# The fifth gate tile of a first SwiGLU, made as a block pair

## The chip, the core and the metric

The kernel runs on one core of one Trainium2 chip. The metric is the device time of one execution in microseconds (us). One execution is also recorded by the hardware profiler; the numbers of engines, lines and instructions below come from that record.

## The reference, cut to what matters

The reference is a network of two layers over 256 latent tokens and 256 context tokens of width 1024, all in 32-bit floats. Each layer has a SwiGLU, a mixer (a short convolution in layer 0, attention in layer 1) and a second SwiGLU, each behind a modulated norm and ahead of a gated residual. The change lies in the first SwiGLU of layer 0:

```python
def _swiglu(h, w13, w2):
    gte, up = jnp.split(h @ w13, 2, axis=-1)
    return (jax.nn.silu(gte) * up) @ w2

lat = lat + 0.5 * mod[:, 0, 2] * _swiglu(_modulate(lat, norm_g[i, 0], ...), ffn_w13[i, 0], ffn_w2[i, 0])
cx = cx + 0.5 * modc[0, 2] * _swiglu(_modulate(cx, norm_g[i, 0], ...), ffn_w13[i, 0], ffn_w2[i, 0])
```

`w13` is 1024 x 5632, `w2` is 2816 x 1024. Latent and context tokens go through the same weights and lie side by side as 512 columns.

## The kernel before, in words

Every 32-bit operand is split into a high part (ScalarE, a copy with rounding) and a low part (VectorE, the source minus the high part). A product is three matmuls: high by high, high weight by low operand, low weight by high operand (`mm3`, L148 to L150 of the profile).

The hidden width is cut into 22 gate tiles of 128, 11 in each half `t` of `ffn`. A tile's weights are 128 x 2048: eight blocks of 128 rows of the contraction, for gate and for up. A tile is made in one of two ways.

**Plain tile.** For each of the 8 contraction blocks, gate and up, three matmuls over all 512 columns: 48 matmuls of 512. Its weights are split in two instructions of 1024 columns on ScalarE and two on VectorE (`load_w`). `w13_post` then makes silu(gate) on ScalarE, the product with up on VectorE, and the two parts of the result.

**Block pair** (class `Pair`). The tile is taken as a 2 x 2 block product (contraction halves by gate and up, against contraction halves by latent and context columns) in Winograd's form with seven products in place of eight: 84 matmuls of 256 columns. It needs weight sums, made by VectorE in the raw weight tile: `sub(0)`, `sub(1)`, `sub(2)` (L804, L809, L811), and four groups of split weights: A (1024 columns), A22 (512), S12 (1024), S34 (1024), each with a ScalarE conversion (L786) and a VectorE one (L789). Of the operand it needs its eight blocks, which are there, and four block sums T1 to T4, split too. In the first SwiGLU they are made once, by `FirstBlocks.sums` (L404 to L411; conversions at L123 and L124), in two pieces of 512 columns each.

The pair loop runs in a fixed order on PE, VectorE and ScalarE (`manual_schedule`): what stands first in the code goes first on its engine. What is written before the loop is placed by the framework's scheduler, which goes by written order among what is ready; `tc.issue_after(x)` adds that an instruction of x's engine comes after x. Iteration `i` of the loop makes, for pair `i`: `head` (products A11 and A12), `five` (S1 by T1), `six` (S2 by T2, S4 by an operand block, then VectorE's add at L847); and for the pair before it `seven` (S3 by T3), which comes between `five` and `six`, and `four` (A22 by T4), which comes last. Among them stand the weights of the next pair: A22 and `sub(0)` after `head`, A and `sub(1)`, `sub(2)` after `seven`, the conversions of S12 and S34 on ScalarE after `six`. The low parts of S12 and S34 are VectorE's first two instructions of the next iteration. ScalarE copies partial results out of the accumulator at L834 (in `head`), L840 (in `five`) and L844 (in `six`).

Split weights lie in four buffers of 1024 columns (`half`), raw weights in two (`load_raw`, filled from SyncE's queue).

In the first SwiGLU, tiles 0 to 2 are made in the hand-ordered start of the kernel, tiles 3 and 4 are plain, and pairs 5 to 10 follow in the loop; the second half `t = 1` is all pairs. `PLAIN` says how many tiles of a SwiGLU are plain. Between their other work the stages also spread 224 "units" of the modulation weights (VectorE, L167, `tick`): `tick(n)` adds n to an account, and each whole one issues a unit. A loop iteration with a pair before it adds `PER_PAIR` = 0.7.

Of the kernel before, what the change touches and what calls it, by code (L numbers as in the profile page):

```python
# [15 lines left out]
ALU = mybir.AluOpType  # L16
# [6 lines left out]
T2 = 2 * S  # L23
NM = 22
NH = NM // 2

PLAIN = {(0, 0): 5, (0, 1): 3, (1, 0): 3, (1, 1): NM}
HEADS = 8
KVH = 2
EPS = 1e-6  # L30
# [18 lines left out]
def hybrid_kernel(ctx: ExitStack, tc: tile.TileContext, a: dict, out: bass.AP):  # L49
    nc = tc.nc  # L50
# [70 lines left out]
    def split(hi, lo, src):  # L121
        return (
            nc.scalar.activation(out=hi, in_=src, func=AF.Copy),  # L123
            nc.vector.tensor_tensor(out=lo, in0=src, in1=hi.bitcast(F32), op=ALU.subtract),  # L124
        )
# [251 lines left out]
    class FirstBlocks(Blocks):  # L377
# [8 lines left out]
        def blk(self, key, k):  # L386
            if key[0] == "B":
                return self.h.at(4 * key[1] + k, key[2] * S, key[2] * S + S)
            return super().blk(key, k)

        def sums(self):
            r = self.raw
            tt = nc.vector.tensor_tensor
            for key in ("T1", "T2", "T3", "T4"):
                self.t[key] = hot("th"), hot("tl")

            def keep(key, q, src):
                hi, lo = self.t[key]
                c = slice(q * T2, q * T2 + T2)
                split(hi[:, c], lo[:, c], src)  # L400

            b = lambda hf, s, q: r[2 * hf + q, s]
            for q in range(2):
                tt(out=b(0, 0, q), in0=b(0, 1, q), in1=b(0, 0, q), op=ALU.subtract)  # L404
                keep("T1", q, b(0, 0, q))
            for q in range(2):
                tt(out=b(0, 1, q), in0=b(1, 1, q), in1=b(0, 1, q), op=ALU.add)
                tt(out=b(1, 1, q), in0=b(1, 1, q), in1=b(0, 0, q), op=ALU.add)
                keep("T2", q, b(1, 1, q))
            for q in range(2):  # L410
                tt(out=b(1, 0, q), in0=b(1, 0, q), in1=b(1, 1, q), op=ALU.subtract)  # L411
                keep("T3", q, b(0, 1, q))
            for q in range(2):
                keep("T4", q, b(1, 0, q))

    def new_pair(s):

# [290 lines left out]
    def w13_post(pp, g, c0, c1):  # L708
        n = c1 - c0
        sg = tp.tile([P, T2], F32, name=nm("sg"), tag="sg", bufs=3)  # L710
        nc.scalar.activation(out=sg[:, :n], in_=pp[0][:, :n], func=AF.Silu)
        gm = tp.tile([P, T2], F32, name=nm("gm"), tag="gm", bufs=3)
        nc.vector.tensor_tensor(out=gm[:, :n], in0=sg[:, :n], in1=pp[1][:, :n], op=ALU.mult)
        split(g[0][:, c0:c1], g[1][:, c0:c1], gm[:, :n])
# [36 lines left out]
    class Pair:  # L751
# [34 lines left out]
            nc.scalar.activation(out=self.shaped(g, 0), in_=self.part(g), func=AF.Copy)  # L786

        def lo(self, g):
            nc.vector.tensor_tensor(  # L789
                out=self.shaped(g, 1), in0=self.part(g), in1=self.shaped(g, 0).bitcast(F32),  # L790
                op=ALU.subtract,
            )
# [177 lines left out]
    def ffn(l, b, h, gate, norm, gs=(), ev=1.5, bd=None):  # L970
        gs = list(gs)
        i0 = 0
        n = NH
        for t in range(2):
            between = ()
            with tc.manual_schedule(engines=set(QUEUES[:3])) if bd else nullcontext():
                if bd:
                    gs, first, post = border_ffn(l, b, h, bd)
                for i in range(len(gs), PLAIN[l, b] if t == 0 and not bd else 0):
                    w = load_w(a["w13"][l, b, i])  # L980
                    pp = psum("pg"), psum("pu")
                    w13_mm(pp, w, h, range(KT), 0, T2)
                    gs.append(new_pair("g"))
                    w13_post(pp, gs[-1], 0, T2)
                    if "T1" not in h.t:
                        with tc.issue_after(begun[-1].ins):
                            h.sums()
                i1 = PLAIN[l, b] if bd else len(gs)
                prs = {i1: first} if bd else {}

                def pair(i):
                    if i not in prs and i < n:
                        prs[i] = Pair(a["w13"][l, b, i0 + i], h)
                    return prs.get(i)

                if not bd:
                    pair(i1).both("A")
                    pair(i1).sums(0)
                    pair(i1).sums(1)
                pair(i1 + 1)  # L1000
                prev = done = None
                if bd:
                    prev = post
                with nullcontext() if bd else tc.manual_schedule(engines=set(QUEUES[:3])):
                    for i in range(i1, n):
                        pr, nxt = pair(i), pair(i + 1)
                        if i > i1:
                            pr.lo("S12")
                            pr.lo("S34")
                        elif bd:  # L1010
                            pr.lo("S12")
                            pr.hi("S34")
                            pr.lo("S34")
                        pair(i + 2)
                        ask_ahead()
                        if prev:
                            prev.silu()
                        pr.head()
                        if done:
                            done.gate()  # L1020
                        if nxt:
                            nxt.both("A22")
                            nxt.sub(0)
                        if done:
                            done.gate_parts()
                        if not nxt:
                            tick(1)
                        if bd and i == i1:
                            h.hi("T4")
                            h.lo("T4")  # L1030
                        pr.five()
                        if prev:
                            tick(0 if bd and i == i1 else PER_PAIR if nxt else PER_PAIR + 1)
                            prev.seven()
                        if nxt:
                            nxt.both("A")
                            nxt.sub(1)
                            nxt.sub(2)
                        pr.six()
                        if nxt:  # L1040
                            nxt.hi("S12")
                            nxt.hi("S34")
                        if prev:
                            gs.append(new_pair("g"))
                            prev.four(gs[-1])
                        done, prev = prev, pr
                prev.silu()
                done.gate()
                done.gate_parts()
            bd = None  # L1050

            def last():
                gs.append(new_pair("g"))
                prev.four(gs[-1])
                prev.gate()
                prev.gate_parts()

            between = prev.seven, last
            i0 += n
            raws2 = {}  # L1060

            def ws2(m):
                for i in range(m, min(m + 2, KT)):
                    if i not in raws2:
                        raws2[i] = load_raw(a["w2h"][l, b, t, i], n * P)
                hs = []
                for c0, c1 in ((0, 6 * P), (6 * P, n * P)):
                    hi, lo = half()
                    hs.append((hi, lo))
                    split(hi[:, : c1 - c0], lo[:, : c1 - c0], raws2[m][:, c0:c1])  # L1070

                def at(k):
                    o = (k % 6) * P
                    return tuple(t[:, o : o + P] for t in hs[k // 6])

                return at

            cur = gs
            end = t == 1
            out = project(  # L1080
                ws2, lambda k, c0, c1: (cur[k][0][:, c0:c1], cur[k][1][:, c0:c1]), n,
                gate, ev, between, norm if end else None,
            )
            gs = []
        return out

    h = Plain()
# [263 lines left out]
    with tc.manual_schedule(engines=set(QUEUES)):  # L1351
# [28 lines left out]
        for i in range(3):  # L1380
# [6 lines left out]
            out=sb1, in0=modb[:, 0, KT : 2 * KT], scalar1=1.0, scalar2=None, op0=ALU.add  # L1387
# [100 lines left out]
        for ch in HALVED:  # L1488
            b = modb[:, :, ch * KT : ch * KT + KT]
# [3 lines left out]
    h = FirstBlocks(h, h32)  # L1493
# [5 lines left out]
    bd = ffn(0, 0, h, gate_at(0, 0), (0, 1, hn), gs0, 3.3)  # L1499
    h = hn  # L1500
# [42 lines left out]
    for m in range(KT):  # L1543
# [12 lines left out]
        if m == 0:  # L1556
# [4 lines left out]
            out=d, in0=u, scalar1=convk[:, 1, m : m + 1], scalar2=None, op0=ALU.mult  # L1561
# [4 lines left out]
            out=d2[:, :, 1:], in0=u2[:, :, : S - 1], scalar=convk[:, 0, m : m + 1],  # L1566
            in1=d2[:, :, 1:], op0=ALU.mult, op1=ALU.add,
        )
        nc.vector.scalar_tensor_tensor(
            out=d2[:, :, : S - 1], in0=u2[:, :, 1:], scalar=convk[:, 2, m : m + 1],  # L1570
            in1=d2[:, :, : S - 1], op0=ALU.mult, op1=ALU.add,
# [20 lines left out]
    h = Blocks()  # L1592
# [764 lines left out]
```

## Time and profile before

| | |
|---|---|
| device time, median of 3 runs | 1546.12 us (1545.3 to 1546.77) |
| device time of the profiled execution | 1545.29 us |
| its span, first to last instruction | 1543.4 us |
| PE matmul busy | 1537.9 us (100%) |
| VectorE busy | 1312.7 us (85%) |
| ScalarE busy | 762.9 us (49%) |
| granted TensorE clock | 1.000 |

Matmuls are pipelined: a matmul of 256 columns shows 283 ns although the next one starts earlier, so rates are read from starts and not from durations. Rows of the timeline give start, duration, engine, line, operation, output <- inputs and shape; a bracket at the end is the idle time of the engine before the row and what ended it. `x2` is two instructions merged into a row.

### The profile page before, as it was taken

What the parts mean: (1) busy time and instruction counts of PE and PEld (TensorE: products, weight loads), DVE (VectorE), ACT (ScalarE), POOL (GpSimd) and SP (SyncE); (2) the same over time, 40 slices, a digit from 0 to 9 for tenths busy, and PEclk for the clock granted to TensorE, in tenths of its full rate; (3) what the DMA queues carried; (4) which work ended last, traced back from release to release, by engine and by line L of the source; (5) the groups of instructions that cost most, each with busy time, mean ns of one, the idle gap of its engine ahead of it and who ended that gap; (6) DMA issues with size and microseconds to landing.
All of it is one profiled execution on the core that took longest, in us unless ns stands there. A gap on an engine that the chain in (4) does not pass through costs nothing.

```text
span 1543.4 us, 25345 instructions
## 1 busy us (share of the span) xinstructions
PE 1537.9 (100%) x10250; PEld 1413.6 (92%) x10250; DVE 1312.7 (85%) x1955; ACT 762.9 (49%) x1286; POOL 28.9 (2%) x24
## 2 busy tenths in 40 slices
PE   9999999999999999999999999999999999999999
PEld 7899899989888899988999899988999899998888
DVE  6988889988988799987998989987998877887663
ACT  5554255536223375532554485522554465775551
POOL 0000000000000000000000000000000002220000
PEclk9999999999999999999999999999999999999999
DMA  9434633354565423355333633356334744255561
GB/s 359 137 111 131 214 120 123 123 197 159 191 199 197 164 90 116 115 183 194 124 124 129 214 117 115 115 182 236 133 132 171 267 143 132 103 182 193 189 227 70
DMA packets 52005, 247.72 MB, mean 160 GB/s; under 512 B 6064, under 2 KB 9264, under 8 KB 36656
## 3 DMA queue, kind: packets, MB, share of 16 engines
q1 hardware_dynamic: 51600, 245.91, 46.9%
q8 instruction: 80, 1.31, 0.3%
q14 instruction: 37, 0.30, 0.1%
q10 hardware_dynamic: 288, 0.19, 0.0%
HBM read 243.72 MB, written 1.05 MB: 159 GB/s over the span
## 4 chain that ended last, share of the span: by engine, by line
PE 91%; DVE 4%; DMA 2%; issue 1%; ACT 0%; DVEq 0%; ACTq 0%
PE py L148 9%; PE py L149 9%; PE py L150 9%; PE p L148 7%; PE p L150 7%; PE p L149 7%; PE q L150 5%; PE q L148 5%; PE q L149 5%; PE py L2015 3%; PE pu L2015 3%; PE pg L2015 3%; DMA wm<-in_modT 2%; DVE junk L167 2%; DVE wl L124 1%
## 5 line engine op out<-in xcount | busy, mean ns | idle before, releaser
L167 DVE CUSTOM_DVE_ANT_0 junk<-wm,scbc,cst 128x1024 bf16<-128x1024 f32 x224 | 286.8, 1280 | 35.4 <-DMA wm<-in_modT 33.5
L123 ACT ACTIVATE wh<-wr 128x1024 fp32r<-128x1024 f32 (+1 forms) x196 | 177.1, 924 | 204.6 <-PE py L149 129.5
L124 DVE TENSOR_TENSOR wl<-wr,wh 128x1024 fp32r<-128x1024 f32 (+1 forms) x196 | 205.2, 1058 | 41.6 <-PE pg L2015 14.3
L148 PE MATMUL py<-gh,wh 128*128 128x512 f32 (+1 forms) x594 | 217.8, 367 | 0.0
L149 PE MATMUL py<-gl,wh 128*128 128x512 f32 (+1 forms) x594 | 217.3, 366 | 0.0
L150 PE MATMUL py<-gh,wl 128*128 128x512 f32 (+1 forms) x594 | 217.1, 365 | 0.0
L786 ACT ACTIVATE wh<-wr 128x1024 fp32r<-128x1024 f32 x165 | 169.5, 1056 | 85.4 <-DVE wr L809 62.9
L789 DVE TENSOR_TENSOR wl<-wr,wh 128x1024 fp32r<-128x1024 f32 x165 | 196.6, 1216 | 16.0 <-ACT wh L786 16.0
L150 PEld LDWEIGHTS py<-gh,wl 128*128 128x128 f32 x594 | 112.0, 189 | 18.0
L148 PEld LDWEIGHTS py<-gh,wh 128*128 128x128 f32 x594 | 112.1, 189 | 17.5
L149 PEld LDWEIGHTS py<-gl,wh 128*128 128x128 f32 x594 | 112.1, 189 | 17.3
L150 PE MATMUL p<-th,wl 128*128 128x256 f32 x440 | 124.5, 283 | 0.0
L149 PE MATMUL p<-tl,wh 128*128 128x256 f32 x440 | 124.5, 283 | 0.0
L148 PE MATMUL p<-th,wh 128*128 128x256 f32 x440 | 124.5, 283 | 0.0
L148 PE MATMUL q<-bh,wh 128*128 128x256 f32 x304 | 86.0, 283 | 0.0
L149 PE MATMUL q<-bl,wh 128*128 128x256 f32 x304 | 86.0, 283 | 0.0
L150 PE MATMUL q<-bh,wl 128*128 128x256 f32 x304 | 86.0, 283 | 0.0
L148 PEld LDWEIGHTS p<-th,wh 128*128 128x128 f32 x440 | 84.5, 192 | 0.2
L149 PEld LDWEIGHTS p<-tl,wh 128*128 128x128 f32 x440 | 84.5, 192 | 0.2
L150 PEld LDWEIGHTS p<-th,wl 128*128 128x128 f32 x440 | 84.5, 192 | 0.0
L804 DVE TENSOR_TENSOR wr<-wr 128x1024 f32<-128x1024 f32 x55 | 67.4, 1225 | 1.7
L150 PE MATMUL q<-th,wl 128*128 128x256 f32 x220 | 62.9, 286 | 0.0
(392 smaller groups left out, 4083.4 us busy)
## 6 DMA issues: line engine op xcount, KB each, us to landing
wr<-in_w SPq DMA_DIRECT2D x85, 1024.0 KB, 4.8
wm<-in_modT SPq DMA_DIRECT2D x128, 512.0 KB, 4.3
wr<-in_w2h SPq DMA_DIRECT2D x48, 704.0 KB, 4.3
wr<-in_cw_cx SPq DMA_DIRECT2D x8, 1024.0 KB, 5.0
wr<-in_w2l SPq DMA_DIRECT2D x8, 1024.0 KB, 4.9
mr<-in_mod SPq DMA_DIRECT2D x8, 512.0 KB, 9.1
wr<-in_cw_b SPq DMA_DIRECT2D x4, 1024.0 KB, 6.2
wr<-in_cw_out SPq DMA_DIRECT2D x4, 1024.0 KB, 5.5
```

Source lines behind the costliest of these rows:

```text
L123: nc.scalar.activation(out=hi, in_=src, func=AF.Copy),
L124: nc.vector.tensor_tensor(out=lo, in0=src, in1=hi.bitcast(F32), op=ALU.subtract),
L148: nc.tensor.matmul(ps, wh, mh, start=first, stop=False, **kw)
L149: nc.tensor.matmul(ps, wh, ml, start=False, stop=False, **kw)
L150: nc.tensor.matmul(ps, wl, mh, start=False, stop=last, **kw)
L167: nc.vector.tensor_tensor_reduce(out=junk, in0=raw, in1=scbc[:, v, :], scale=0.5 if ch in HALVED else 1.0, scalar=modb[:, l, col : col + 1 ...
L786: nc.scalar.activation(out=self.shaped(g, 0), in_=self.part(g), func=AF.Copy)
L789: nc.vector.tensor_tensor(out=self.shaped(g, 1), in0=self.part(g), in1=self.shaped(g, 0).bitcast(F32), op=ALU.subtract,)
L804: tt(out=by_two(raw[:, :1024]), in0=a21.unsqueeze(1).to_broadcast([P, 2, T2]), in1=by_two(raw)[:, :, :T2], op=ALU.subtract,)
L2015: nc.tensor.matmul(p[:, :n], w(j, k)[part], m(k)[:, :n], start=not part and k == 0, stop=part == 1 and k == nk - 1, skip_group_check=True,)
```

## The change

Tile 4 becomes a pair, so that tile 3 is the only plain tile left and the loop runs over pairs 4 to 10. The block sums are taken apart: `sums` keeps T1 and T2, `sum3` has the two pieces of T3, `sum4` those of T4 with their subtraction. Ahead of the loop the order is now: T1, T2; the weights of pair 4; tile 3's silu; T3, whose VectorE part comes after the low part of pair 4's S34; the rest of tile 3's post-processing after that. T4 is made inside the loop, in its first iteration (`i == i1`), between `sub(2)` of the next pair and `six`. The host lays out the weights of tile 4 as a pair's.

```diff
-PLAIN = {(0, 0): 5, (0, 1): 3, (1, 0): 3, (1, 1): NM}
+PLAIN = {(0, 0): 4, (0, 1): 3, (1, 0): 3, (1, 1): NM}
...
+        def keep(self, key, q, src):
+            hi, lo = self.t[key]
+            c = slice(q * T2, q * T2 + T2)
+            return split(hi[:, c], lo[:, c], src)[1]
...
+        def sum3(self):
             for q in range(2):
-                tt(out=b(1, 0, q), in0=b(1, 0, q), in1=b(1, 1, q), op=ALU.subtract)
-                keep("T3", q, b(0, 1, q))
+                self.made = self.keep("T3", q, self.raw[q, 1])
+
+        def sum4(self):
+            b = lambda hf, s, q: self.raw[2 * hf + q, s]
             for q in range(2):
-                keep("T4", q, b(1, 0, q))
+                nc.vector.tensor_tensor(
+                    out=b(1, 0, q), in0=b(1, 0, q), in1=b(1, 1, q), op=ALU.subtract
+                )
+                self.keep("T4", q, b(1, 0, q))
...
         def lo(self, g):
-            nc.vector.tensor_tensor(
+            self.made = nc.vector.tensor_tensor(
...
-                    w13_post(pp, gs[-1], 0, T2)
                     if "T1" not in h.t:
                         with tc.issue_after(begun[-1].ins):
                             h.sums()
+                    post = Post(pp)
+                    post.four(gs[-1])
...
                     pair(i1).sums(1)
+                    if post:
+                        post.silu()
+                        with tc.issue_after(pair(i1).made.ins):
+                            h.sum3()
+                        with tc.issue_after(h.made.ins):
+                            post.gate()
+                            post.gate_parts()
...
                             nxt.sub(1)
                             nxt.sub(2)
+                        if post and i == i1 and not bd:
+                            h.sum4()
                         pr.six()
```

More of the change, by code (lines that the diff above doesn't have):

```diff
@@ L389, in blk @@
             return super().blk(key, k)
+        def keep(self, key, q, src):
+            hi, lo = self.t[key]
+            c = slice(q * T2, q * T2 + T2)
+            return split(hi[:, c], lo[:, c], src)[1]
         def sums(self):
-            r = self.raw
+            r, keep = self.raw, self.keep
             tt = nc.vector.tensor_tensor
@@ L395, in sums @@
                 self.t[key] = hot("th"), hot("tl")
[L397 to L400, printed above, removed]
             b = lambda hf, s, q: r[2 * hf + q, s]
@@ L974, in ffn @@
         for t in range(2):
-            between = ()
+            between, post = (), None
             with tc.manual_schedule(engines=set(QUEUES[:3])) if bd else nullcontext():
```

## The prediction

> **What bounds the kernel now.** I read the page first, then the list of PE's waits, then the timeline of the first SwiGLU engine by engine. From the page, the engines, the modulation unit and the weight load:
>
> ```profile
> PE 1537.9 (100%) x10250; PEld 1413.6 (92%) x10250; DVE 1312.7 (85%) x1955; ACT 762.9 (49%) x1286; POOL 28.9 (2%) x24
> ...
> L167 DVE CUSTOM_DVE_ANT_0 junk<-wm,scbc,cst 128x1024 bf16<-128x1024 f32 x224 | 286.8, 1280 | 35.4 <-DMA wm<-in_modT 33.5
> ...
> wr<-in_w SPq DMA_DIRECT2D x85, 1024.0 KB, 4.8
> ```
>
> All waits of PE on another engine:
>
> ```profile
> PE idle L1093 <- DVE eps_t L105: 1.1, 1, 1.1
> PE py L149 <- DVE zl L124: 0.6, 1, 0.6
> PE cs L1285 <- ACT table L1098: 0.4, 1, 0.4
> ```
>
> PE waits 2.1 us in 1543.4. The kernel is a row of matmuls, and a change is worth the matmul time that it removes, less every wait that it puts into the row. The two ways of making a tile, as two stretches of the timeline (stretch, length, PE, PEld, DVE, ACT, POOL, granted clock, DMA): plain tile 3, and pair 5 with one product too few and the next pair's first products:
>
> ```profile
> 58.33:69.21 10.88, 10.88 (x50) 9.01 (x49) 10.88 (x18) 6.53 (x12) 0.00 (x0) 1.00 0.25 93
> 80.08:90.16 10.08, 10.08 (x86) 10.07 (x84) 8.33 (x10) 6.12 (x11) 0.00 (x0) 1.00 0.33 106
> ```
>
> A plain tile is 48 matmuls in 10.88 us, 0.2267 us each; 84 matmuls of 256 columns take 10.08 us, 0.120 us each. So the change can win 10.88 - 10.08 = 0.80 us, 0.05% of the time, and no more. The rest is the question whether VectorE (DVE) and ScalarE (ACT) still deliver in time. The place to look is the loop's first pair and its successor, today pairs 5 and 6. PE at the head of pair 6 and at its third product, S1 by T1:
>
> ```profile
> 87.28 0.28 PE L148 MATMUL p<-hh,wh 128*128 128x256 f32 x1
> ...
> 90.16 0.28 PE L148 MATMUL q<-th,wh 128*128 128x256 f32 x1
> 90.28 0.28 PE L149 MATMUL q<-tl,wh 128*128 128x256 f32 x1
> 90.48 0.39 PE L150 MATMUL q<-th,wl 128*128 128x256 f32 x1
> 90.70 0.28 PE L148 MATMUL q<-th,wh 128*128 128x256 f32 x1
> ```
>
> The third matmul, the first that reads the low part of S12, starts 0.20 us after the second and the next 0.22 us later, where 0.12 is the rule: 0.18 us are lost, too little for the list of waits. The low part of S12 comes at the very moment it is needed. VectorE and ScalarE ahead of it:
>
> ```profile
> 80.52 1.23 DVE L789 TENSOR_TENSOR wl<-wr,wh 128x1024 fp32r<-128x1024 f32 x1 [4.16 <-ACT wh L786]
> ...
> 86.02 1.23 DVE L789 TENSOR_TENSOR wl<-wr,wh 128x1024 fp32r<-128x1024 f32 x1 [0.88 <-ACT wh L786]
> 87.28 0.69 DVE L809 TENSOR_TENSOR wr<-wr 128x512 f32<-128x512 f32 x1
> 88.00 0.69 DVE L811 TENSOR_TENSOR wr<-wr 128x512 f32<-128x512 f32 x1
> 88.61 0.68 DVE L847 TENSOR_TENSOR sg<-q,sg 128x512 f32<-128x512 f32 x1
> 89.21 2.35 DVE L789 TENSOR_TENSOR wl<-wr,wh 128x1024 fp32r<-128x1024 f32 x2
> ```
>
> ```profile
> 84.65 0.38 ACT L840 COPY gm<-q 128x256 f32<-128x256 f32 x1 [1.46 <-PE q L150]
> 84.92 1.06 ACT L786 ACTIVATE wh<-wr 128x1024 fp32r<-128x1024 f32 x1
> 86.04 0.38 ACT L844 COPY sg<-p 128x256 f32<-128x256 f32 x1
> 88.06 2.01 ACT L786 ACTIVATE wh<-wr 128x1024 fp32r<-128x1024 f32 x2 [1.65 <-DVE wr L809]
> ```
>
> The rows stand in the order of the code: copy out of `five`, A of pair 6, `sub(1)`, `sub(2)`, the add of `six`, S12, S34. A cannot come earlier, because ScalarE's copy at 84.65 waits for PE to finish `five`; so the low part of A (86.02 to 87.25) ends at the head of pair 6 (87.28), and the chain from it to S12 leaves nothing over.
>
> **The change part by part.** *PE.* Tile 4's 48 matmuls go, pair 4's 84 come: -0.80 us, all on the path.
>
> *T4 in the loop.* This is the step with a price. In the first iteration it stands after `sub(2)`, ahead of the add and of S12: per piece a subtraction, a ScalarE conversion, a low part that waits for it. The trace has the three in a row elsewhere, a gate product and its parts, on DVE and on ACT; and the T3 and T4 pieces themselves, with tile 4's weights behind them:
>
> ```profile
> 138.99 0.69 DVE L866 TENSOR_TENSOR gm<-sg,p 128x512 f32<-128x512 f32 x1 [0.41 <-PE p L150]
> 140.37 0.69 DVE L124 TENSOR_TENSOR gl<-gm,gh 128x512 fp32r<-128x512 f32 x1 [0.70 <-ACT gh L123]
> ```
>
> ```profile
> 139.71 0.63 ACT L123 ACTIVATE gh<-gm 128x512 fp32r<-128x512 f32 x1 [1.33 <-DVE gm L866]
> ```
>
> ```profile
> 64.39 0.68 DVE L411 TENSOR_TENSOR hr<-hr,hr 128x512 f32<-128x512 f32 x1
> 64.99 1.89 DVE L124 TENSOR_TENSOR tl<-hr,th 128x512 fp32r<-128x512 f32 x3
> 66.79 2.35 DVE L124 TENSOR_TENSOR wl<-wr,wh 128x1024 fp32r<-128x1024 f32 x2
> ```
>
> From subtraction to low part 1.38 us (138.99 to 140.37), from there to the next instruction 0.60 (64.39 to 64.99): 1.98 us a piece, and the second piece's subtraction stands behind the first's low part, so two pieces take 3.96 us. ScalarE gives nearly the same: the conversion of S12, today 0.78 us after `sub(1)` starts (87.28 to 88.06), now stands behind the second T4 conversion and the copy of L844. That is 0.72 + 0.61 to the first subtraction, 1.98 for its piece, 0.72 to the second conversion, 0.53 for it (0.63 less about 0.1 by which back-to-back conversions overlap, 2 x 1.06 - 2.01), 0.27 for the copy (84.65 to 84.92): 4.83 us. The conversion takes 1.06 and the low part follows 0.04 later, at 5.93 us after `sub(1)` starts, today at 1.93 (87.28 to 89.21): 4.00 us later. I take 4.0. Nothing covers it, since today's margin is below nothing by 0.08 us; PE waits some 3.1 us for the high part of S12, makes two matmuls, and waits 0.9 more for the low part. Behind that instruction on PE stand all other products; `seven` and `four` find T3, T4 and S34 ready. Bounds: if the conversions hid, 4 VectorE steps of 0.60, 2.4 us; upwards, what follows.
>
> *The entry to the loop.* T1, T2 and pair 4's weights must be ready. Tile 3 ends at 69.21, and pair 5's head follows 60 matmuls later, at 76.41, as today from 80.08 to 87.28. The removed pieces of T3 and T4 (six steps of 0.60) and tile 4's two low parts (2.35) give VectorE about 6 us ahead of 69.2; A, A22, S12 and the subtractions of pair 4 take 1.14 + 0.6 + 1.14 + 0.7 + 0.7 + 1.14, 5.4. S34 needs a weight buffer of tile 3, as A of pair 5 does now:
>
> ```profile
> 68.56 1.06 ACT L786 ACTIVATE wh<-wr 128x1024 fp32r<-128x1024 f32 x1 [2.83 <-PE pg L149]
> 69.53 0.57 ACT L711 ACTIVATE sg<-pg 128x512 f32<-128x512 f32 x1
> ```
>
> So S34's low part runs from 69.66 to 70.8, then T3 (1.2), tile 3's product (0.6), A22 of pair 5 (0.6), tile 3's low part (0.6 with 0.2 of waiting), `sub(0)` (1.14): to 75.1. By ScalarE, A's low part can start 1.62 us after `five` ends (84.40 to 86.02), at 73.53 + 1.62 = 75.15. Both come out equal, so the entry costs nothing, or up to 0.7 us if the scheduler places tile 3's conversion or T3's later than I have it. Each such microsecond is added to the 4.0. S4 of pair 4 needs S34 at 75 and has it 4 us before.
>
> *Buffers and queues.* T3 and T4 issue no transfer. Pair 6's raw weights wait for S34 of pair 4 (70.8, today tile 4's at 69.1), land 4.8 us later (the page's row) and are asked for after 79. Pair 7's land at about 90, are asked for after 91. The raw operand stays some 15 us longer in buffers that nobody asks for before the eighth gate result. Nothing.
>
> *The account of units.* One more iteration has a predecessor: 0.7 more, so one unit comes ahead of the rest from here on and other places get 3 for 4 or 4 for 3. A unit is 1.28 us of VectorE. Counted through the code, the same 92 units precede the last z of the convolution in both kernels, one fewer inside that stage; the 0.6 us that PE waits there for zl can go, or up to 1.28 us appear at some other place. I take 0, with -0.6 and +1.3 as ends.
>
> Sum: -0.80 + 4.0 + 0 + 0 = +3.2 us. Against the profiled execution that is 1545.29 + 3.2 = 1548.5 (1543.4 of span and 1.9 around it). It lies 0.83 us under the median of the runs, and the same step from the median gives 1549.3.
>
> **The rivals.** *The written order is not what runs* (not slower). If T4's six instructions ran behind S12 and S34 of pair 5, they would be due only for `four`, eight products later, and PE would wait for nothing: -0.80, 1545.3. It decides at 4 us of slack ahead of S12. Against it: all rows above keep the written order within the loop. 0.08.
>
> *Half of it hides.* If the conversions cost VectorE nothing, only its four steps count: -0.8 + 2.4 = +1.6, 1547.7. For it, ACT has 1.65 us of idle there; against it, VectorE waits 0.70 for the conversion in the row at 140.37. 0.12.
>
> *VectorE enters late.* If T3's conversions or tile 3's parts are queued badly, A and S12 slip by 0.5 to 1.3 more: +3.7 to +4.5, about 1550.2. For it, my two sums for A meet within 0.1 us. 0.20.
>
> *PE slows down after the wait.* At the start PE's matmuls come at lower density for some time, at the same granted clock:
>
> ```profile
> 2.00:3.00 1.00, 1.00 (x7) 1.00 (x6) 0.00 (x0) 0.99 (x2) 0.00 (x0) 1.00 0.78 202
> ...
> 5.00:6.00 1.00, 1.00 (x11) 0.98 (x9) 0.97 (x3) 0.98 (x2) 0.00 (x0) 1.00 1.07 420
> ```
>
> 7 in place of 11 in a microsecond over about 4 us loses 4 x (1 - 7/11) = 1.5 us. After the 0.4 us wait of the list nothing of the kind shows; the trace has no wait of 3 us. If 3.1 us are enough: +4.7, 1550.8. 0.10. [...]
>
> **How the numbers follow.** The forecast has 0.50: +3.2, with 1548.6 to 1550.3 for the entry and the units. With the rivals the range that leaves out 2 in 10 reaches from 1547.4 (the half-hidden case, less a little) to 1551.2 (both upper rivals). A measurement of this kernel can tell about 0.2%, 3.1 us, from no change: below 1543.0 faster, above 1549.2 slower. Faster needs four times what the matmuls can give: 0.02. Slower takes a little over half of the forecast, most of the late entry and the slow PE: 0.28 + 0.16 + 0.09 = 0.53. Same 0.45.
>
> **What would show it.** In the changed profile: tile 3 to the head of pair 4 without a gap; the first two products of pair 5 on time at about 76.4; then on PE a wait of 3 us and one of 1 us at S1 by T1 of pair 5, released by ACT L786 and DVE L789; on DVE in that iteration two rows of L411's kind with 0.7 us of waiting behind each, at about 78 to 82; pair 6 on time relative to pair 5. Wrong if PE shows no wait there, if a wait stands at the head of pair 5 (A, not S12), or if the time moves elsewhere in the kernel.

## The result, and the profile after

| | before | after |
|---|---|---|
| median, 8 runs each on one chip | 1546.13 us (1545.3 to 1547.33) | 1550.74 us (1549.06 to 1552.46) |
| ratio | | 1.0031, 95% interval 1.0021 to 1.0040 |
| profiled execution, span | 1545.29, 1543.4 us | 1552.46, 1550.6 us |
| granted TensorE clock over the span | 1.000 | 0.997 (0.997 to 0.999 in the eight runs) |

The change costs 4.6 us. The profiled execution after is the slowest of its eight, so its parts are read one by one and not added up to the median.

PE's waits after the change, all of them (engine, output and line, what it waited for: total us, times, longest):

```profile
PE q L148 <- ACT wh L792: 2.9, 1, 2.9
PE idle L1109 <- DVE eps_t L105: 1.1, 1, 1.1
PE py L149 <- DVE zl L124: 0.7, 1, 0.7
PE py L150 <- DVE wl L124: 0.6, 1, 0.6
PE q L150 <- DVE wl L795: 0.5, 1, 0.5
```

The first and the last are new and are S12 of pair 5, high part and low part. The fourth, in the convolution, is not in the list of before either; the units come back to it. VectorE in the loop's first iteration, from the low part of A of pair 5 on (the lines have moved: L815 and L817 are `sub(1)` and `sub(2)`, L417 is T4's subtraction, L853 the add of `six`):

```profile
75.39 1.23 DVE L795 TENSOR_TENSOR wl<-wr,wh 128x1024 fp32r<-128x1024 f32 x1
76.65 0.69 DVE L815 TENSOR_TENSOR wr<-wr 128x512 f32<-128x512 f32 x1
77.38 0.69 DVE L817 TENSOR_TENSOR wr<-wr 128x512 f32<-128x512 f32 x1
77.99 0.69 DVE L417 TENSOR_TENSOR hr<-hr,hr 128x512 f32<-128x512 f32 x1
79.37 0.69 DVE L124 TENSOR_TENSOR tl<-hr,th 128x512 fp32r<-128x512 f32 x1 [0.70 <-ACT th L123]
79.98 0.69 DVE L417 TENSOR_TENSOR hr<-hr,hr 128x512 f32<-128x512 f32 x1
81.36 0.69 DVE L124 TENSOR_TENSOR tl<-hr,th 128x512 fp32r<-128x512 f32 x1 [0.69 <-ACT th L123]
81.97 0.68 DVE L853 TENSOR_TENSOR sg<-q,sg 128x512 f32<-128x512 f32 x1
82.58 2.36 DVE L795 TENSOR_TENSOR wl<-wr,wh 128x1024 fp32r<-128x1024 f32 x2
```

Here is T4 in the gap, two pieces with 0.70 us of waiting for ScalarE in each. S12's low part starts 5.93 us after `sub(1)` does (76.65 to 82.58); before it was 1.93 (87.28 to 89.21). ScalarE shows the same from its side:

```profile
78.71 0.63 ACT L123 ACTIVATE th<-hr 128x512 fp32r<-128x512 f32 x1 [3.35 <-DVE hr L417]
80.70 0.63 ACT L123 ACTIVATE th<-hr 128x512 fp32r<-128x512 f32 x1 [1.36 <-DVE hr L417]
81.24 0.35 ACT L850 COPY sg<-p 128x256 f32<-128x256 f32 x1
81.49 2.00 ACT L792 ACTIVATE wh<-wr 128x1024 fp32r<-128x1024 f32 x2
```

And PE at the same place, from the last matmul of pair 5's `head`:

```profile
79.40 0.28 PE L150 MATMUL q<-hh,wl 128*128 128x256 f32 x1
82.60 0.58 PE L148 MATMUL q<-th,wh 128*128 128x256 f32 x1 [2.92 <-ACT wh L792]
82.98 0.42 PE L149 MATMUL q<-tl,wh 128*128 128x256 f32 x1
83.86 0.58 PE L150 MATMUL q<-th,wl 128*128 128x256 f32 x1 [0.46 <-DVE wl L795]
84.24 0.42 PE L148 MATMUL q<-th,wh 128*128 128x256 f32 x1
84.45 0.42 PE L149 MATMUL q<-tl,wh 128*128 128x256 f32 x1
...
88.72 0.30 PE L148 MATMUL p<-th,wh 128*128 128x256 f32 x1
88.86 0.28 PE L149 MATMUL p<-tl,wh 128*128 128x256 f32 x1
```

The third matmul was due at 79.76 (79.40 and three steps of 0.12) and starts at 83.86: 4.1 us late. What follows is the second thing to see: the starts are 0.21 us apart and not 0.12, until 88.7. The windows name the cause in their third column from the right, the granted clock:

```profile
80.00:82.00 2.00, 0.00 (x0) 0.00 (x0) 1.30 (x4) 1.30 (x3) 0.00 (x0) 0.98 0.00 0
82.00:84.00 2.00, 0.94 (x3) 0.65 (x3) 2.00 (x4) 2.00 (x4) 0.00 (x0) 0.50 0.00 0
84.00:86.00 2.00, 2.00 (x10) 2.00 (x11) 1.97 (x3) 0.81 (x3) 0.00 (x0) 0.50 0.21 25
86.00:88.00 2.00, 2.00 (x11) 2.00 (x11) 0.80 (x1) 1.33 (x2) 0.00 (x0) 0.50 0.85 283
88.00:90.00 2.00, 2.00 (x16) 2.00 (x15) 1.06 (x2) 0.00 (x0) 0.00 (x0) 0.81 0.55 225
90.00:92.00 2.00, 2.00 (x19) 2.00 (x19) 1.93 (x4) 1.11 (x2) 0.00 (x0) 1.00 0.00 0
```

Half clock from about 81.92 to 88.76, 6.8 us (worked out from 0.98 and 0.81). The 22 matmuls from 83.86 to 88.72 took 4.86 us; at 0.12 each, with the 0.10 that PE loses at a restart (90.48 to 90.70 in the kernel before, 0.22 in place of 0.12), it would be 2.74. By this estimate the clock cost 2.1 us in this execution.

### The profile page after: what moved, and what is told of

Same layout as the page of the kernel before. It is cut to its first block, busy times and chain, and to the rows that moved or that the text cites. A ratio compares the mean times of both kernels' runs of the same rounds, so it can differ in the third digit from the quotient of the medians.

```text
span 1550.6 us, 25419 instructions
## 1 busy us (share of the span) xinstructions
PE 1541.3 (99%) x10286; PEld 1418.3 (91%) x10286; DVE 1317.8 (85%) x1962; ACT 765.2 (49%) x1291; POOL 28.9 (2%) x24
## 4 chain that ended last, share of the span: by engine, by line
PE 89%; DVE 6%; DMA 3%; issue 2%; ACT 1%; DVEq 0%; ACTq 0%
PE py L148 9%; PE py L149 9%; PE py L150 9%; PE p L148 7%; PE p L149 7%; PE p L150 7%; PE q L150 5%; PE q L148 5%; PE q L149 5%; PE py L2031 3%; PE pu L2031 3%; PE pg L2031 3%; DMA wm<-in_modT 2%; DVE junk L167 2%; DVE wl L124 1%
## 5 line engine op out<-in xcount | busy, mean ns | idle before, releaser
L792 ACT ACTIVATE wh<-wr 128x1024 fp32r<-128x1024 f32 x168 | 172.7, 1056 | 85.8 <-DVE wr L815 76.4
L795 DVE TENSOR_TENSOR wl<-wr,wh 128x1024 fp32r<-128x1024 f32 x168 | 200.4, 1218 | 9.6 <-ACT wh L792 9.5
L148 PE MATMUL q<-th,wh 128*128 128x256 f32 x224 | 64.1, 286 | 2.9 <-ACT wh L792 2.9
```

The lines of the kernel that those rows point to most:

```text
L148: nc.tensor.matmul(ps, wh, mh, start=first, stop=False, **kw)
L795: self.made = nc.vector.tensor_tensor(out=self.shaped(g, 1), in0=self.part(g), in1=self.shaped(g, 0).bitcast(F32), op=ALU.subtract,)
```

## The experiments

Ratios are against the kernel before, run in turns with it on the same chip. The kernels of the first four ran together (before: 1545.25 us), those of the next four together (1544.95 us), the last alone (1545.60 us); each group had a chip of its own. "Over before" is the difference of the medians; the ratio is estimated from the runs by itself, and the two differ by up to 0.7 us. Over such a span, 3.4 us at half clock show as a clock of 0.999, 6.8 us as 0.998.

| kernel | median us | over before | ratio, 95% interval | clock of the runs |
|---|---|---|---|---|
| T4 moved behind S12 | 1544.03 | -1.2 | 0.9990, 0.9982 to 0.9999 | 1.000 in 10 of 11 |
| units kept in place | 1550.10 | +4.9 | 1.0027, 1.0016 to 1.0038 | 0.998 to 0.999 |
| both | 1544.26 | -1.0 | 0.9994, 0.9986 to 1.0002 | 1.000 in 11 of 12 |
| before + two T4 pieces | 1551.34 | +6.1 | 1.0035, 1.0023 to 1.0047 | 0.997 to 0.999 |
| after, wait filled | 1547.92 | +3.0 | 1.0014, 1.0005 to 1.0023 | 1.000 in all 11 |
| after, T4 in another order | 1548.16 | +3.2 | 1.0016, 1.0007 to 1.0025 | 0.999 in 9 of 11 |
| before + one T4 piece | 1548.24 | +3.3 | 1.0019, 1.0010 to 1.0028 | 0.999 in 4 of 11 |
| before + three T4 pieces | 1553.47 | +8.5 | 1.0055, 1.0043 to 1.0068 | 0.997 to 0.998 |
| before + one, first wait filled | 1546.58 | +1.0 | 1.0008, 0.9999 to 1.0017 | 1.000 in all 11 |

The kernel before is not free of clock falls either: in 4 of its 66 runs in these groups the clock is 0.997 or 0.998. None of those runs was profiled. The profile of three pieces has more of it than the fall in the loop: a clock of 0.997 over its span of 1551.4 us takes some 7.8 us or more at half clock (2 x 0.0025 x 1551.4), the loop's fall lasts 6.8, and the rest lies outside the windows from 88 to 106 us.

**T4 moved behind S12.** Theory: the place of T4 is the whole loss. Rival: the extra pair is more than VectorE can carry. In the diffs, `late` is the loop's second iteration.

```diff
-                        if post and i == i1 and not bd:
-                            h.sum4()
...
                             pr.lo("S34")
+                        if late:
+                            h.sum4_sub()      # T4's two subtractions
...
                             nxt.sub(0)
+                        if late:
+                            h.sum4_parts()    # T4's conversions
```

> The changed kernel with T4 taken out of the gap ahead of pair 5's S12: its subtractions stand behind the low part of S34 of pair 5, its conversions behind sub(0) of pair 6, in the loop's second iteration. Theory (T4's place delays S12 by 4.0 us, PE then runs at half clock for a while, and the shift of the modulation units costs 1.2 us more): the 4.0 and the clock go, the units stay: 0.3 to 0.6 us above the kernel before, about 1546.5, no PE wait over 0.3 us in the loop and the granted clock at 1.00 throughout. Rival (an extra pair is more than VectorE can carry, wherever T4 stands): PE waits 1 to 4 us later in the loop, 1548 to 1550.

VectorE in the second iteration (S12 and S34 of pair 5, then T4, A22 and `sub(0)` of pair 6, T4's low parts):

```profile
77.87 0.68 DVE L856 TENSOR_TENSOR sg<-q,sg 128x512 f32<-128x512 f32 x1
78.47 2.35 DVE L798 TENSOR_TENSOR wl<-wr,wh 128x1024 fp32r<-128x1024 f32 x2
80.74 1.28 DVE L417 TENSOR_TENSOR hr<-hr,hr 128x512 f32<-128x512 f32 x2
81.94 0.68 DVE L798 TENSOR_TENSOR w4l<-wr,w4h 128x512 fp32r<-128x512 f32 x1
82.66 1.23 DVE L813 TENSOR_TENSOR wr<-wr 128x1024 f32<-128x1024 f32 x1
83.80 1.29 DVE L124 TENSOR_TENSOR tl<-hr,th 128x512 fp32r<-128x512 f32 x2
```

VectorE runs through without a wait: the conversions on ScalarE lie beside A22 and `sub(0)`. S12's low part follows `sub(2)` and the add as it did before the change. The list of PE's waits holds a single entry, the 1.1 us at the kernel's start. So VectorE carries the extra pair, and the pair is a gain, if a narrow one: 1.2 us under the kernel before, with an interval of -2.8 to -0.2 us, and by the two ratios about 6 us under the changed one. That interval holds the -0.8 of the matmuls but is too wide to measure it. The profiles do: from tile 3's first matmul to S1 by T1 of pair 8 PE takes 52.17 us before (58.33 to 110.50) and 51.59 here (58.47 to 110.06), 0.58 us less. The missing 0.2 is lost ahead of A22 by T4 of pair 4, whose first two steps take 0.24 and 0.23 us (85.24, 85.48, 85.71) in place of 0.12: too short for the list of waits. The 0.3 to 0.6 above the kernel before that was expected, for the units, was wrong.

**Units kept in place.** The account starts 0.7 lower, so that the extra iteration moves no unit:

```diff
-    owed = [0.0]
+    owed = [-PER_PAIR]
```

> The changed kernel, with the account of modulation units started at -0.7, so that each unit stands where it stood before the change. Theory: the 0.6 us wait for the second weight tile of the convolution's output and the smaller losses behind the first SwiGLU go: 1.0 to 1.4 us under the changed kernel, about 1549.5; the wait at S1 by T1 stays at 3 us and 1 us. Rival (the later losses are only scatter of that execution or come from the shifted start of the stage): no difference to the changed kernel.

No gain: +4.9 us here and +4.6 for the changed kernel, one inside the interval of the other. Behind the loop, this kernel issues the same instructions in the same order as the kernel before on VectorE and SyncE, and yet its profile lacks the 0.6 us wait for zl which that one shows:

```profile
PE q L148 <- ACT wh L792: 2.9, 1, 2.9
PE idle L1109 <- DVE eps_t L105: 1.1, 1, 1.1
PE cs L1301 <- ACT table L1114: 0.7, 1, 0.7
PE q L150 <- DVE wl L795: 0.5, 1, 0.5
```

So one order of instructions gave the wait for zl in one profiled execution and not in the other. The rival fits: these waits (0.6 us before; 0.7 and 0.6 after) are scatter, and the account of units costs nothing that these runs can measure.

**Both.**

> Both edits together: T4 out of the gap and the units where they were. Theory: only the matmul saving is left, -0.8 us, with the 0.2 us that was lost at pair 6 before either gone or moved: 1545.2 to 1545.6, 0.5 to 0.9 us under the kernel before. Rival (VectorE cannot carry the extra pair): above the kernel before.

-1.0 us (interval -2.2 to +0.3); it cannot be told from the version with the units shifted, which says the same of the units once more.

**The kernel before with two pieces of T4's kind.** The delay alone, without the change: at the same place of the first iteration, with n = 2,

```diff
                             nxt.sub(2)
+                        if t == 0 and isinstance(h, FirstBlocks) and i == i1:
+                            h.again(n)
```

where each piece is `b = max(b, b)` on VectorE and its two parts made again.

> The kernel before, plain tile and all, with two idempotent pieces put into its first loop iteration at the place where the change puts T4: each takes the maximum of a raw T4 piece with itself on VectorE and makes its two parts again. It adds T4's delay and nothing else. Theory: PE waits 3 us and 1 us at S1 by T1 of pair 6, +4.0 us, then runs at half clock for some microseconds, +0.3 to +2.3: 1550.3 to 1552.5. Rival (half of the six instructions hides): +2.4, 1548.5. Rival (no clock drop without the rest of the change): +4.0 with the granted clock at 1.00.

```profile
PE q L148 <- ACT wh L794: 3.0, 1, 3.0
PE q L150 <- DVE wl L797: 0.8, 1, 0.8
```

(The two entries of the list that are new.) The plain tile is there, the saving is not, and the loss is the same wait and the same clock. Six small instructions in that place cost 6.1 us.

**After, wait filled.** It tests the clock by itself: PE is given matmuls that nobody needs while it waits.

```diff
+                        if post and not bd and i == i1 + 1:
+                            keep_on = psmall("idle")
+                            for _ in range(13):
+                                nc.tensor.matmul(
+                                    keep_on[:, :P], ident, ident, start=True, stop=True
+                                )
                         pr.five()
```

> The changed kernel with 13 matmuls of the constant identity with itself (128 columns, into an accumulator that nobody reads) put on PE in the loop's second iteration between head and five, where PE waits 3.1 us for S12. They take about 2.7 us and so lie inside the wait; they are extra work, left out of no result. Theory (the changed kernel pays 4.0 us of waiting and about 1.5 us for a clock that the idle gap halves): the granted clock stays at 1.00, the wait for S12 is otherwise as it was, and the time is about 3.1 us over the kernel before, 1.5 under the changed kernel. Rival (the halved clock has another cause, or costs nothing at the end): as the changed kernel, +4.6.

```profile
79.12 3.06 PE L1048 MATMUL idle<-cst 128*128 128x128 f32 x26
82.19 0.39 PE L148 MATMUL q<-th,wh 128*128 128x256 f32 x1
82.42 0.28 PE L149 MATMUL q<-tl,wh 128*128 128x256 f32 x1
83.45 0.39 PE L150 MATMUL q<-th,wl 128*128 128x256 f32 x1 [0.76 <-DVE wl L795]
83.67 0.28 PE L148 MATMUL q<-th,wh 128*128 128x256 f32 x1
83.79 0.28 PE L149 MATMUL q<-tl,wh 128*128 128x256 f32 x1
```

(The 13 matmuls are 26 instructions in the trace.) The products are as late as in the changed kernel (the third matmul due at 79.36, started at 83.45: 4.1 us), but they then go at 0.12, and the clock is 1.000 in every run. +3.0 us in place of +4.6: useless work on PE gains 1.6 us, which is the price of the halved clock. The two figures come from different groups and their intervals overlap (+0.8 to +3.6 and +3.2 to +6.2), so this alone gives the price only roughly; the kernel with one piece, below, gives 1.5 within its own runs.

**After, T4 in another order.** Both subtractions first, then the conversions, in the same place.

> The changed kernel with T4 in the same place, but both subtractions first and then the two conversions: the second subtraction no longer stands behind the first low part. By the rows S12 is then 2.6 us late and not 4.0, PE's first wait 1.7 us. Theory: +1.8 us over the kernel before with the granted clock at 1.00; if a gap of 1.7 us is enough to halve the clock, +3.3. Rival (the delay is set by the number of instructions and not by the chain through ScalarE): no difference to the changed kernel.

```profile
78.19 1.29 DVE L417 TENSOR_TENSOR hr<-hr,hr 128x512 f32<-128x512 f32 x2
79.58 1.29 DVE L124 TENSOR_TENSOR tl<-hr,th 128x512 fp32r<-128x512 f32 x2
80.79 0.68 DVE L856 TENSOR_TENSOR sg<-q,sg 128x512 f32<-128x512 f32 x1
```

The two pieces take 2.60 us (78.19 to 80.79) in place of 3.98 (77.99 to 81.97), so a third of the delay was the order within T4. The time is +3.2: by the wait alone it would be +1.8, and the clock still falls, although PE's two waits are only 1.5 and 0.8 us here:

```profile
82.00:84.00 2.00, 1.33 (x6) 1.33 (x7) 2.00 (x3) 1.62 (x4) 0.00 (x0) 0.58 0.00 0
84.00:86.00 2.00, 2.00 (x12) 2.00 (x12) 1.58 (x2) 0.78 (x2) 0.00 (x0) 0.57 0.66 111
86.00:88.00 2.00, 2.00 (x19) 2.00 (x18) 1.06 (x2) 0.55 (x1) 0.00 (x0) 1.00 1.01 422
```

Half clock for about 3.4 us, half as long as after the change.

**One piece, three pieces.** The same edit as for two.

> The kernel before with one idempotent T4 piece at that place. Theory: S12 is 2.0 us late, PE waits about 1.0 and 0.9 us, no gap is long enough for the clock: +2.0 us, clock 1.00. Rival (any gap of 1 us costs clock too): +3.5.

> The kernel before with three idempotent T4 pieces at that place. Theory: S12 is 6.0 us late, PE waits 5.1 and 0.9 us, the clock halves: +6.0 and 2 to 3 us for the clock, +8 to +9. If the clock's cost came from the number of T4 pieces or from VectorE's backlog and not from PE's gap, it would grow by half: +9 to +10; if there were no such cost, +6.

Three pieces: +8.5, as expected, with a wait of 5.1 us and, in the loop, the clock at half for 6.8 us. One piece: +3.3, and the clock does fall in 4 of 11 runs, the profiled one among them. PE's two waits there were 1.0 and 0.8 us, and the clock fell 3 us after the first began, when PE was running again:

```profile
90.00:92.00 2.00, 0.81 (x5) 0.40 (x3) 1.95 (x3) 2.00 (x4) 0.00 (x0) 1.00 0.00 0
92.00:94.00 2.00, 1.46 (x9) 1.46 (x10) 2.00 (x3) 1.49 (x4) 0.00 (x0) 0.80 0.00 0
94.00:96.00 2.00, 2.00 (x11) 2.00 (x11) 1.45 (x2) 1.33 (x2) 0.00 (x0) 0.50 0.63 188
```

I had expected no fall there. Within this kernel the four runs with a fall have a median of 1548.8 us and the seven without 1547.3: 1.5 us for a fall, and +2.4 us without one, near the expected +2.0. Three readings were left: the short gaps add up, or the first or the second one does it alone.

**One piece, first wait filled.** Four matmuls in the first gap, the second gap left as it is.

> The kernel before with one idempotent T4 piece in its first loop iteration, and four matmuls of the identity with itself on PE ahead of five of the next iteration, so that the first of the two waits for S12 (1.0 us) is filled and the second (0.8 us) is left; the added work changes no result. Theory (short gaps add up within a stretch of some 3 us, and about 2 us of idle in it halve the clock): with 0.8 us of idle the clock stays at 1.00 in every run and the time is +2.0 us over the kernel before, 1.3 under the kernel with the unfilled piece. Rival (the 0.8 us gap does it alone): the granted clock falls to 0.999 in part of the runs and the median stays at +3.

The clock stays at 1.000 in all 11 runs, as it did in the 11 runs of "after, wait filled", which keep a gap of 0.8 us too. So a gap of 0.8 us alone was not enough in 22 runs. A first gap of 1.0 us without the second was not run, so it is not shown whether the first does it alone or the two add up. The time is +1.0, less than the 2.0 that PE is late in its profile; the interval (-0.2 to +2.6 us) holds both.

## Why the prediction was right or wrong

The sign, the range and the place were right; the likeliest time was not. Forecast were +3.2 us and 1549.3, measured +4.6 and 1550.74, which is the rival "PE slows down after the wait" (+4.7, 1550.8), to which the text gave 0.10.

*Matmuls, -0.80 us.* The version with T4 moved away shows the gain nearly alone: -1.2 with an interval that holds it, and in its profile 0.58, with 0.2 lost elsewhere. Right.

*T4 in the loop, 4.0 us.* Forecast from rows of the kernel before: S12's low part 5.93 us after the start of `sub(1)`. The row after: 76.65 to 82.58, 5.93. ScalarE's conversion of S12 at 4.83; the row: 76.65 to 81.49, 4.84. The wait came in its two parts, 3 us and then the low part, where it was said. The changed kernel with the clock kept up is +3.0, the sum was +3.2. Right, and shown by taking it away (-1.2) and by adding it alone (the same two waits, +6.1 with the clock).

*The entry to the loop, nothing.* The low part of A starts at 75.39 against a forecast 75.15, with everything 0.23 us later in that execution (pair 5's head at 76.64 against 76.41). Right; "VectorE enters late" did not occur.

*The account of units, 0.* Not contradicted, against my own reading after the first profile, where I put 1.2 us of the later waits to it. The two kernels with the units kept showed no gain; an effect of a few tenths of a microsecond would not show in their intervals.

*The clock.* This step failed: the forecast put it at nothing. I had seen its price in the slow start of the profile (1.5 us; measured 1.6), but took 3.1 us for too short a gap; that was my estimate, and the trace, in which PE's longest wait is 1.1 us, did not show it. The clock fell in every run of the kernels with a gap of 3 us (8 of 8, 6 of 6, 6 of 6), in 9 of 11 with 1.5 and 0.8 us, in 4 of 11 with 1.0 and 0.8. A sum with the clock in it, -0.8 + 4.0 + 1.5 = +4.7, would have been right to 0.1 us, but that is partly luck. The 7 and 11 of the prediction count every matmul that touches the microsecond; by their starts, the first 14 matmuls take 3.15 us (1.06 to 4.21, mostly 0.21 apart) where the later 0.11 would make 1.6, which gives about the same loss. And the start is about 3 us of steady work at half rate, while the half clock in the profile after lasts 6.8 us, of which PE waits for more than 1. Nor is it shown that the start was "at the same granted clock": the trace's records of the clock begin at 4.23 us, where the starts change from 0.21 to 0.11 us apart, and the 1.00 that the windows print ahead of it is no measurement.

*Half of it hides.* Refuted: both conversions are waited for in full (0.70 and 0.69 us).

## What to carry to other kernels

Before work is put into a loop in fixed order, find the row at which the bounding engine takes its operand at the last moment; whatever was written ahead of that operand here cost its full chain, the ping-pong between two engines included: 4.0 us. The same work behind that operand cost 0.2 us here, and the change was then a small gain. And a wait can cost more than its length: the clock fell in every run in which PE waited 3 us, in 9 of 11 with waits of 1.5 and 0.8 us close together and in 4 of 11 with 1.0 and 0.8, which added 1.6 us to 3.0 after the change and 1.5 to 2.4 with one piece.

## What the runs showed of the hardware

Four profiles show the fall of the clock in the loop by their windows, which give the granted clock as 0.50 between fall and rise. The third column is what PE was busy in the 3.4 us ahead of the fall, which is as long as the shorter of the half clocks:

| kernel | clock falls at, us | PE busy in the 3.4 us ahead, us | half clock lasts, us |
|---|---|---|---|
| before + three | 94.1 | 1.1 | 6.8 |
| after | 81.9 | 1.2 | 6.8 |
| after, T4 in another order | 82.3 | 1.5 | 3.4 |
| before + one | 93.2 | 1.7 | 3.4 |

In the first two the clock fell within PE's first wait (5.1 and 2.9 us), in the third within the second (1.5, then 0.8 us). With one piece (1.0, then 0.8 us) PE was running again when it fell: nine matmuls start between 92.00 and 94.00. What decided between 3.4 and 6.8 us is not shown, nor why the clock fell in part of the runs of the last two kernels (9 and 4 of 11), since one execution of each was profiled.

Matmuls that nobody needs, put into the gap, kept the clock at 1.000 in 22 of 22 runs: 13 in the gap of 3 us, 4 in that of 1.0. In the profiles of these two kernels PE is idle for 0.76 us from 82.00 to 84.00 and for 0.84 us from 90.00 to 94.00, so it was busy for at least 2.6 of any 3.4 us there (an estimate, 3.4 less 0.84). PE's waits are not the whole of it: the kernel before, whose longest wait in the profiled execution is 1.1 us, had a clock of 0.997 or 0.998 in 4 of its 66 runs.

An unchanged order of instructions gave a wait of 0.6 us in the convolution in one profiled execution and none in another. On a kernel of 1545 us whose runs mostly spread by 2 to 4 us, a single profile is not enough to charge such a wait to an edit.
